# A hybrid two-layer trunk: x scaled token by token before its transpose, and the modulation vector summed in columns

## The chip, the cores and the metric

The kernel runs on one core of one Trainium2 chip. The metric is the device time of one execution in microseconds (us); lower is better. One core has TensorE (PE; its weight loads are listed as PEld), VectorE (DVE), ScalarE (ACT), GpSimd (POOL) and SyncE (SP), and each of them runs its own instructions in order and waits on semaphores for the others. DMA transfers are issued from the queues of SP, ACT and POOL.

## What is computed

One sequence of 1024 tokens by 1024 channels goes through two layers. Only the first half of layer 0, up to its attention, is touched:

```python
def ada(c, w_ada, b_ada):                 # six vectors of 1024 each
    return (silu(c) @ w_ada + b_ada)      # w_ada: 1024 x 6144
h = rms_norm(x, norm_mix) * (1 + scale) + shift
p = h @ w_in                              # 1024 x 2048: S5 | q | k | v
u = p[..., :512]                          # diagonal state-space model (S5), then a GLU
q, k, v = ...                             # 512 each: 4 heads, differential attention,
                                          # q and k normed per 64 channels and rotated
x = x + gate * (concat(s5, attention) @ w_out)
```

The first two of the six modulation vectors (shift and scale of the mixer) are needed before h; the other four (its gate, and those of the FFN) only later. All matrix products are fp32 in effect: each operand is split in a high part that TensorE takes in one pass (fp32r, names ending in hi) and the rest (lo), and a product is hi·hi + hi·lo + lo·hi, three matmuls.

## The kernel before

Activations lie channel-major: a tile `x[b]` holds 128 channels by 8 groups and 512 tokens of block b. `start` (L1071) is the first phase. `load_x` (L347) brings x in eight tiles of 128 tokens, transposes each on TensorE in 128x128 pieces (`xps`), copies the result to x (half on VectorE, half on ScalarE) and squares the token-major tile on ScalarE for the RMS sums. `mods_row` (L265) computes the first 2048 columns of the modulation as rows: the vector silu(c) is the stationary operand, one column, and 512 columns of `w_ada` stream past it (`mpr`); the four rows are copied, transposed back (`mpc`) and added to the bias (`mod`, L291), and `gm` (L302) is the norm's gain times 1 + scale. `scaled` (L1089) multiplies x by the token's 1/rms, spread over partitions through TensorE (`bc`), and `shifted` (L1095) makes `nh` = gm·xn + mod on ScalarE, its cast m0hi and its rest m0lo on VectorE. Beside it `s5_params` (L592) works out the S5 discretisation: exponentials and sines on small tiles, then powers of the 64 states by complex products (`cmul`, L678 to L683; `s5E` on VectorE, `s5D` on GpSimd), then a table `s5W` on GpSimd (L772 to L777), stored through SP's queue to `dR`, and short products `s5gp`, `s5kp` on TensorE.

`u_proj` (L1118) multiplies the first 512 columns of w_in in four blocks of 128, each for two token blocks: 24 matmuls of 128x512 for one `pu`. Weights come as 512 KB tiles `wraw`, are cast on ScalarE (`whi`, L449) and their rest is made on VectorE (`wlo`, L450). Then `attn_proj` (L914) runs twice, for two pairs of heads: for q, k and v, eight tiles `pq` of 128 tokens by 256 columns, 24 matmuls each. A q or k tile is squared (`asq`, ScalarE), summed by head (`ass`, VectorE), raised to -1/2 (`ars`, GpSimd), multiplied out of PSUM (`aqn`, L952), rotated on GpSimd and transposed (`tq`). pu and pq share two PSUM buffers. S5 quarters (`pS`, `H`, `pY`) are woven into the first attn_proj, the first attention steps (`sps`, `mx`, `po`, `os`) into the second.

The remaining 4096 modulation columns take another road, `mods_acc` (L310): a tile `mwt` of w_ada rows is multiplied by silu(c) per partition and accumulated on VectorE (`macc`, L334 and L336) over eight tiles, and TensorE sums over the partitions with a vector of ones (`mpc`, L391). 2048 of these columns stand beside u_proj in tiles of 1024, and 2048 beside the second attn_proj in tiles of 512, with two mwt buffers each.

In this part of the kernel the order on each engine is not the program's: a scheduler places the instructions by its own estimate of times, with the program's order as its preference, and may hoist one past others when its buffers are free. `weave(a, b, r)` in the program interleaves r steps of b with each step of a, `chain` runs one after the other, `lockstep` one step of each in turn. From the FFN on the order of TensorE is fixed by hand.

## Time and profile before

| | us |
|---|---|
| median of three runs | 3184.99 (3182.13 to 3188.43) |
| the profiled execution | 3195.05 |
| its span | 3192.2 |
| TensorE busy in the span | 2998.9 (94%) |
| VectorE, ScalarE, GpSimd busy | 1940.1, 1157.8, 891.2 |
| TensorE busy, 0 to 416 us | 341.10 |

The mean granted TensorE clock of the execution is 0.971 of full speed (2.4 GHz; the lower of its two levels is 1.2 GHz, a granted clock of 0.5). The chain of work that ended last is TensorE for 40% of the span and VectorE for 4%. Over the whole span TensorE is the busy engine, so an idle stretch of it is what can be won, and the first 416 us hold 75 of the 193 us of them.

A row of a timeline reads: start, duration, engine, line, operation, tile written and tiles read, count of like instructions that follow each other, and in brackets how long the engine stood idle before and for what. A wait for several things is put down to the last. A row of a group ("lines") gives the busy time, the mean of one in ns, and the idle time ahead.

### The profile page before, as it was taken

To read this page: it belongs to the slowest core of one execution; us is meant where nothing else is said; L and a number is where in the kernel's file an instruction comes from. 1 tells how busy PE (TensorE), PEld (TensorE's weight loads), DVE (VectorE), ACT (ScalarE), POOL (GpSimd) and SP (SyncE) were. 2 spreads that over 40 slices of the span, in tenths; PEclk is the share of its full clock that TensorE was granted. 3 is DMA by queue.
4 is the path that set the end of the run, shared out by engine and by line. 5 is a ranking of instruction groups with operands and counts; after the bars stand their busy time and mean duration, and the time that the engine had idled before them with its cause. 6 is when DMAs were issued, how large, how long until landed. Compare 5 with 4: busy or idle time off the path is not lost. (4 is left out here: it accounts for less than half of the span.)

```text
span 3192.2 us, 51849 instructions
## 1 busy us (share of the span) xinstructions
PE 2998.9 (94%) x19966; PEld 2242.3 (70%) x19966; DVE 1940.1 (61%) x3918; ACT 1157.8 (36%) x2318; POOL 891.2 (28%) x1002
## 2 busy tenths in 40 slices
PE   5889999998999999999999999999999999999998
PEld 2678866776777766666666777666766667777777
DVE  6854665556674646777777456467777774434443
ACT  3212443333223644343333245433434432322222
POOL 6652411001111302443443342034444334200000
PEclk7889998999999999999999999999999999999999
DMA  7753221224574442221222254422222213523332
GB/s 248 189 151 67 80 73 53 83 71 145 176 219 134 147 150 88 71 68 57 80 79 62 81 165 133 153 68 72 76 62 79 74 54 93 168 86 94 96 103 92
DMA packets 489862, 338.44 MB, mean 106 GB/s; under 512 B 44280, under 2 KB 451088, under 8 KB 488592
## 3 DMA queue, kind: packets, MB, share of 16 engines
q1 hardware_dynamic: 474288, 304.75, 32.0%
q0 software_dynamic: 7632, 25.64, 2.6%
q10 hardware_dynamic: 7696, 4.74, 0.6%
q8 instruction: 158, 2.59, 0.3%
q14 instruction: 88, 0.72, 0.1%
HBM read 292.59 MB, written 42.47 MB: 105 GB/s over the span
## 5 line engine op out<-in xcount | busy, mean ns | idle before, releaser
L449 ACT CAST whi<-wraw 128x1024 fp32r<-128x1024 f32 (+2 forms) x472 | 401.8, 852 | 897.8 <-PE pu L466 180.8
L466 PE MATMUL pd<-dd,whi 128*128 128x512 f32 x1408 | 463.3, 410 | 12.8 <-DVE x L534 7.8
L450 POOL TENSOR_TENSOR wlo<-wraw,whi 128x1024 fp32r<-128x1024 f32 (+2 forms) x184 | 325.0, 1767 | 491.0 <-ACT whi L449 467.4
L450 DVE TENSOR_TENSOR wlo<-wraw,whi 128x1024 fp32r<-128x1024 f32 (+2 forms) x288 | 298.1, 1036 | 267.6 <-ACT whi L449 252.1
L466 PE MATMUL pg<-fhi,whi 128*128 128x512 f32 x704 | 302.2, 429 | 13.4 <-DVE sg L521 10.8
L466 PEld LDWEIGHTS pd<-dd,whi 128*128 128x128 f32 x1408 | 253.8, 189 | 79.2 <-ACT whi L449 17.2
L466 PE MATMUL pu<-fhi,whi 128*128 128x512 f32 x704 | 296.4, 421 | 1.3 <-ACT ev L1360 0.6
L466 PE MATMUL pg<-fhi,wlo 128*128 128x512 f32 x704 | 282.9, 402 | 6.9 <-DVE wlo L450 6.9
L466 PE MATMUL pu<-fhi,wlo 128*128 128x512 f32 x704 | 279.8, 397 | 4.0 <-POOL wlo L450 2.4
L466 PE MATMUL pg<-flo,whi 128*128 128x512 f32 x704 | 281.9, 400 | 0.0
L466 PE MATMUL pd<-dd,wlo 128*128 128x512 f32 x704 | 279.2, 397 | 1.9 <-DVE oss L1053 1.0
L466 PE MATMUL pu<-flo,whi 128*128 128x512 f32 x704 | 278.5, 396 | 0.0
L534 DVE SCALAR_TENSOR_TENSOR x<-pd,mod,x 128x512 f32<-128x512 f32 x192 | 143.4, 748 | 123.4 <-PE pd L466 122.3
L466 PE MATMUL pkrv<-xh,whi 128*128 128x512 f32 x384 | 164.3, 428 | 12.6 <-ACT ev L1360 6.8
L466 PEld LDWEIGHTS pg<-fhi,whi 128*128 128x128 f32 x704 | 134.9, 192 | 48.6 <-DVE sg L521 12.0
L466 PEld LDWEIGHTS pg<-fhi,wlo 128*128 128x128 f32 x704 | 135.1, 192 | 40.8 <-DVE wlo L450 9.4
L466 PEld LDWEIGHTS pd<-dd,wlo 128*128 128x128 f32 x704 | 133.1, 189 | 38.4 <-DVE wlo L450 5.5
L466 PEld LDWEIGHTS pu<-fhi,whi 128*128 128x128 f32 x704 | 133.0, 189 | 37.1 <-issue 2.4
L466 PEld LDWEIGHTS pu<-fhi,wlo 128*128 128x128 f32 x704 | 133.0, 189 | 36.1 <-POOL wlo L450 3.3
L466 PE MATMUL pkrv<-xh,wlo 128*128 128x512 f32 x384 | 153.5, 400 | 2.0 <-DVE wlo L450 2.0
L466 PEld LDWEIGHTS pg<-flo,whi 128*128 128x128 f32 x704 | 135.5, 192 | 25.2
L466 PE MATMUL pkrv<-xl,whi 128*128 128x512 f32 x384 | 153.1, 399 | 0.0
(457 smaller groups left out, 6026.0 us busy)
## 6 DMA issues: line engine op xcount, KB each, us to landing
wraw<-in_ffn_w_gate SPq DMA_DIRECT2D x88, 512.0 KB, 3.9
wraw<-in_ffn_w_up SPq DMA_DIRECT2D x88, 512.0 KB, 4.0
wraw<-in_ffn_w_down SPq DMA_DIRECT2D x128, 256.0 KB, 2.7
...
kd<-ev SPq DMA_DIRECT2D x48, 256.0 KB, 2.0
...
```

What stands on the lines that cost most here:

```text
L449: nc.scalar.copy(hi, raw)
L450: (eng or nc.vector).tensor_tensor(lo, raw, hi.bitcast(F32), op=ALU.subtract)
L466: nc.tensor.matmul(out, lhsT=w(k), rhs=x(k), start=first and i == 0, stop=last and i == n - 1)
L534: nc.vector.scalar_tensor_tensor(x[:, n, :], pd, gate[:, n : n + 1], x[:, n, :], op0=ALU.mult, op1=ALU.add)
```

## The change

- `mods_row` turns its product round: pieces of w_ada of 128 rows by 128 columns are the stationary operand and silu(c) is one moving column, 128 products (two passes each) into 16 columns of one PSUM tile. The four row copies, the four transposes and the strided sum are replaced by one sum.
- `load_x` also scales the token-major tile in place by the token's 1/rms: a small operation on VectorE (`nrs`), a pow on GpSimd (`nrp`) and a scaled copy on ScalarE for each of eight tiles. `scaled`, with its 16 multiplies and the tiles xn, is dropped.
- `shifted` transposes the scaled tiles a second time (`xnp`, 64 transposes) and makes m0hi and nh from PSUM with two activations on ScalarE, so that VectorE makes only m0lo.
- `u_proj` runs two column blocks in lockstep; shifted is woven into it, and S5's parameters at one step in two.
- The eight stores of the S5 table go to GpSimd's queue.
- All 4096 later modulation columns are now in tiles of 512 with four buffers: 22 of the 64 steps beside the first attn_proj and the rest beside the second.

```diff
-        pr = self.pa.tile([P, 512], F32, tag="d", name=self.nm("mpr"))
-        row = self.tp.tile([P, 512], F32, tag="ev", name=self.nm("mrow"))
-        nc.gpsimd.memset(row, 0.0)
+        nc = self.nc
+        w = self.A["w_ada"][l]
+        pc = self.pa.tile([P, 16], F32, tag="d", name=self.nm("mpc"))
         for k in range(KT):
             for u in range(2):
                 wt = self.wp.tile([P, 1024], F32, tag=("wraw", "whi", "wlo")[(2 * k + u) % 3], name=self.nm("mwt"))
                 nc.sync.dma_start(wt, w[k * P : (k + 1) * P, u * 1024 : (u + 1) * 1024])
-                for t in range(2):
-                    q = 2 * u + t
+                for q in range(8):
                     nc.tensor.matmul(
-                        pr[32 * q : 32 * q + 1, :],
-                        lhsT=self.cact[:, k : k + 1],
-                        rhs=wt[:, t * 512 : (t + 1) * 512],
-                        start=(k == 0),
-                        stop=(k == KT - 1),
+                        pc[:, 8 * u + q : 8 * u + q + 1], lhsT=wt[:, q * P : (q + 1) * P], rhs=self.cact[:, k : k + 1],
+                        start=(k + u + q == 0), stop=(k == KT - 1), skip_group_check=True,
                     )
             yield
-        for t in range(4):
-            nc.scalar.copy(row[32 * t : 32 * t + 1, :], pr[32 * t : 32 * t + 1, :])
-        pc = self.pa.tile([P, 512], F32, tag="d", name=self.nm("mpc"))
-        for q in range(4):
-            nc.tensor.transpose(pc[:, q * P : (q + 1) * P], row[:, q * P : (q + 1) * P], self.ident)
-        nc.vector.tensor_tensor(
-            self.mod[l][:, 0:16].rearrange("p (t q) -> p t q", q=4),
-            pc.rearrange("p (q t r) -> p t q r", q=4, r=32)[:, :, :, 0],
-            self.vc1[:, 48 * l : 48 * l + 16].rearrange("p (t q) -> p t q", q=4),
-            op=ALU.add,
-        )
+        nc.vector.tensor_tensor(self.mod[l][:, 0:16], pc, self.vc1[:, 48 * l : 48 * l + 16], op=ALU.add)
         self.mods_g(l, 1)
...
             sq = self.tp.tile([P, D], BF16, tag="ev", name=self.nm("xsq"))
             nc.scalar.activation(sq, xi, AF.Square, accum_out=ss[:, t : t + 1])
+            rs = self.cp.tile([P, 1], F32, tag="nrs", name=self.nm("nrs"), bufs=2)
+            nc.vector.tensor_scalar(rs, ss[:, t : t + 1], 1.0 / D, EPS, op0=ALU.mult, op1=ALU.add)
+            rp = self.cp.tile([P, 1], F32, tag="nrp", name=self.nm("nrp"), bufs=2)
+            nc.gpsimd.tensor_tensor(rp, rs, self.mhalf[:, 0:1], op=ALU.pow)
+            nc.scalar.activation(xi, xi, AF.Copy, scale=rp[:, 0:1])
...
             for qt in range(4):
                 for i in range(2):
-                    nc.sync.dma_start(self.dR[qt][:, i], W[i][:, 4 * qt : 4 * qt + 4, :])
+                    g_.dma_start(self.dR[qt][:, i], W[i][:, 4 * qt : 4 * qt + 4, :])
...
-        def scaled(b):
-            bc = self.rstd_rows(self.rstd_pow(self.cp, ss[:, 4 * b : 4 * b + 4], 1.0 / D, EPS))
-            for k in range(KT):
-                v.tensor_tensor(xn[b][:, k, :], x[b][:, k, :], bc, op=ALU.mult)
-                yield
-
         def shifted(b):
 
             hh.append(self.big(F32R, f"m0hi{b}"))
             hl.append(self.big(F32R, f"m0lo{b}"))
             for k in range(KT):
-                t = self.tp.tile([P, TB], F32, tag="t1", name=self.nm("nh"))
-                nc.scalar.activation(
-                    t, xn[b][:, k, :], AF.Identity, bias=self.mod[0][:, k : k + 1], scale=self.gm[0][:, k : k + 1]
-                )
-                v.tensor_copy(hh[b][:, k, :], t)
-                v.tensor_tensor(hl[b][:, k, :], t, hh[b][:, k, :].bitcast(F32), op=ALU.subtract)
+                pt = self.ps.tile([P, TB], F32, tag="mm", name=self.nm("xnp"))
+                for t in range(4):
+                    nc.tensor.transpose(
+                        pt[:, t * P : (t + 1) * P], xt[2 * b + t // 2][:, t % 2, k * P : (k + 1) * P], self.ident
+                    )
+                t1 = self.tp.tile([P, TB], F32, tag="t1", name=self.nm("nh"))
+                for o in (hh[b][:, k, :], t1):
+                    nc.scalar.activation(
+                        o, pt, AF.Identity, bias=self.mod[0][:, k : k + 1], scale=self.gm[0][:, k : k + 1]
+                    )
+                v.tensor_tensor(hl[b][:, k, :], t1, hh[b][:, k, :].bitcast(F32), op=ALU.subtract)
                 yield
 
-        drain(weave(weave(self.mods_row(0), chain(self.load_x(xt, x, ss), scaled(0)), RA), self.some(s5, RF), RB))
+        drain(weave(weave(self.mods_row(0), self.load_x(xt, x, ss), RA), self.some(s5, RF), RB))
         for b in range(NB):
             for i in range(2):
                 nc.sync.dma_start(self.xs[b][:, 4 * i : 4 * i + 4, :], x[b].t[i])
+        self.m0 = hh, hl
+        sh = chain(shifted(0), shifted(1))
         if mix:
-            drain(weave(chain(weave(shifted(0), scaled(1), RD), shifted(1)), s5, RC))
-        if mix:
+            drain(self.some(sh, 2), weave(weave(self.u_proj(self.at, hh, hl), sh, 1), s5, RD))
             self.attn_consts(Scratch(self.page([P, 4 * TB], F32, "atc")))
-        self.m0 = hh, hl
+        else:
+            drain(sh)
...
-        w = {}
-        for n, b in ((0, 0), (1, 0), (0, 1), (1, 1), (2, 0), (2, 1), (3, 0), (3, 1)):
-            if not b:
-                w[n] = self.wsplit(win[:, n * P : (n + 1) * P].rearrange("(k p) n -> p k n", p=P), [P, KT, P])
-            hi, lo = w[n]
-            pu = self.pa.tile([P, TB], F32, tag="d", name=self.nm("pu"))
-            self.mm3(pu, lambda k: hi[:, k, :], lambda k: lo[:, k, :], lambda k: hh[b][:, k, :], lambda k: hl[b][:, k, :], KT)
-            ut = at.tile([P, 8, 64], F32, tag="ut", name=self.nm("ut"), bufs=2)
-            nc.scalar.copy(ut, pu.rearrange("p (c j) -> p j c", j=8))
-            nc.sync.dma_start(self.us[n][:, :, 64 * b : 64 * b + 64], ut)
-            yield
+        for n0 in (0, 2):
+            ws = [
+                self.wsplit(win[:, n * P : (n + 1) * P].rearrange("(k p) n -> p k n", p=P), [P, KT, P]) for n in (n0, n0 + 1)
+            ]
+            for b in range(NB):
+                pus = [self.pa.tile([P, TB], F32, tag="d", name=self.nm("pu")) for _ in ws]
+                yield from lockstep(*(self.mm3w(pu, *w, hh[b], hl[b], KT) for pu, w in zip(pus, ws)))
+                for n, pu in enumerate(pus, n0):
+                    ut = at.tile([P, 8, 64], F32, tag="ut", name=self.nm("ut"), bufs=2)
+                    nc.scalar.copy(ut, pu.rearrange("p (c j) -> p j c", j=8))
+                    nc.sync.dma_start(self.us[n][:, :, 64 * b : 64 * b + 64], ut)
...
-        drain(weave(self.u_proj(at, hh, hl), self.mods_acc(0, (2 * D, 4 * D), self.pz, "z", tiles, nc.sync), MR))
         self.late_vectors()
         hs = self.open("s5h", 1, side="right")
         s5 = chain(*(self.s5_quarter(n, hs) for n in range(4)))
-        drain(weave(self.attn_proj(0, at, self.pa, hh, hl), s5, 1))
+        t0 = [self.tp.tile([P, TB], F32, tag=g, name=self.nm("mwt")) for g in ("t0", "ev") for _ in range(2)]
+        t1 = [self.tp.tile([P, TB], F32, tag="t1", name=self.nm("macc")) for _ in range(2)]
+        it = iter(range(1000))
+
+        def tiles():
+            i = next(it)
+            return t0[i % 4], t1[i // 8 % 2]
+
+        mods = self.mods_acc(0, (2 * D, 6 * D), self.pz, "z", tiles, nc.sync, TB)
+        drain(weave(self.attn_proj(0, at, self.pa, hh, hl), weave(s5, self.some(mods, 22), 1), 2))
         self.close(hs)
         self.attn_pages()
         ap = self.ap = self.open("m0a", 1, side="right")
-        t0 = [self.tp.tile([P, TB], F32, tag="t0", name=self.nm("mwt")) for _ in range(2)]
-        t1 = [self.tp.tile([P, TB], F32, tag="t1", name=self.nm("macc")) for _ in range(2)]
-        it = iter(range(1000))
-
-        def tiles():
-            i = next(it)
-            return t0[i % 2], t1[i // 8 % 2]
-
-        mods = self.mods_acc(0, (4 * D, 6 * D), self.pz, "z", tiles, nc.sync, TB)
-        drain(weave(self.attn_proj(1, at, self.pa, hh, hl), weave(self.attn_steps(0, (0, 1), ap, self.pa), mods, 1.6), 2.2))
+        drain(weave(self.attn_proj(1, at, self.pa, hh, hl), weave(self.attn_steps(0, (0, 1), ap, self.pa), mods, 2), 3))
```

`mm3w` (L457) is the generator that gives the 24 matmuls of a product in eight steps, as before.

On VectorE, before, around the modulation (`mod`, and `gm` made from it), with the S5 powers s5c and s5E:

```order
L683 TENSOR_TENSOR s5E_14_158<-s5c 128x16x16
L1092 TENSOR_TENSOR xn_9_143<-x_1_135,bc_517 128x512 x4
L1092 TENSOR_TENSOR xn_10_144<-x_2_136,bc_517 128x512 x4
L678 TENSOR_TENSOR s5c<-s5E_13_157,s5t_447 128x256
L679 TENSOR_TENSOR s5c<-s5E_14_158,s5t_449 128x256
L291 TENSOR_TENSOR mod_118<-mpc_506,vc_102 128x16
L705 COPY s5B_674<-s5E_14_158 128x512
L680 TENSOR_TENSOR s5E_13_157<-s5c 128x16x16
L302 SCALAR_TENSOR_TENSOR gm_120<-mod_118,vc_102 128x8
```


and now, at the same place:

```order
L667 TENSOR_TENSOR s5c<-s5E_9_153,s5t_577 128x256
L668 TENSOR_TENSOR s5c<-s5E_10_154,s5t_579 128x256
L439 TENSOR_TENSOR wlo_671<-wraw_668,whi_670 128x1024
L669 TENSOR_TENSOR s5E_9_153<-s5c 128x16x16
L670 TENSOR_TENSOR s5c<-s5E_10_154,s5t_577 128x256
L671 TENSOR_TENSOR s5c<-s5E_9_153,s5t_579 128x256
L280 TENSOR_TENSOR mod_118<-mpc_176,vc_102 128x16
L672 TENSOR_TENSOR s5E_10_154<-s5c 128x16x16
L286 SCALAR_TENSOR_TENSOR gm_120<-mod_118,vc_102 128x8
L343 COPY x_4_138<-xps_564 128x4x128
```


What stood behind gm, the rest of the S5 powers and the wlo of the first two u weights, now stands ahead of it.

On TensorE, before, from the last u product to the first q tile (`vp` is a transpose of small vectors):

```order
L466 MATMUL pu_1424<-m0hi_169_1016,wlo_1355 128x512
L466 MATMUL pu_1424<-m0hi_169_1016,whi_1354 128x512
L391 MATMUL mpc_1388<-ones,macc_1139 32x1 x32
L466 MATMUL pu_1424<-m0lo_171_1018,whi_1354 128x512
L466 MATMUL pu_1424<-m0hi_169_1016,wlo_1355 128x512
L466 MATMUL pu_1424<-m0hi_169_1016,whi_1354 128x512
L466 MATMUL pu_1424<-m0lo_171_1018,whi_1354 128x512
L466 MATMUL pu_1424<-m0hi_169_1016,wlo_1355 128x512
L250 MATMUL vp_1499<-ident,vr_1490 128x104
L466 MATMUL pq_1521<-whi_1511,m0hi_104_534 128x256
L466 MATMUL pq_1521<-wlo_1512,m0hi_104_534 128x256
```


and now:

```order
L455 MATMUL pu_1412<-m0hi_140_809,wlo_1204 128x512
L455 MATMUL pu_1413<-m0hi_140_809,whi_1209 128x512
L455 MATMUL pu_1413<-m0lo_142_811,whi_1209 128x512
L455 MATMUL pu_1413<-m0hi_140_809,wlo_1210 128x512
L797 MATMUL pS_1657<-UT_1636,s5E_9_153 64x128 x8
L797 MATMUL pS_1666<-UT_1636,s5E_10_154 64x128 x8
L455 MATMUL pq_1592<-whi_1582,m0hi_111_638 128x256
L455 MATMUL pq_1592<-wlo_1583,m0hi_111_638 128x256
```


The column sums mpc between the u matmuls are gone, and two products pS of the first S5 quarter stand ahead of the first q tile.

On VectorE, before, ahead of the first row sums `ass` of the q tiles:

```order
L336 SCALAR_TENSOR_TENSOR macc_2850<-mwt_2848,cact,macc_2850 128x512
L336 SCALAR_TENSOR_TENSOR macc_1139<-mwt_1138,cact,macc_1139 128x1024
L334 TENSOR_SCALAR macc_1139<-mwt_1138,cact 128x1024
L336 SCALAR_TENSOR_TENSOR macc_1139<-mwt_1138,cact,macc_1139 128x1024
L323 TENSOR_TENSOR mod_118<-mpc_1388,vc_102 128x8
L251 COPY vc_103<-vp_1499 128x104
L450 TENSOR_TENSOR wlo_1518<-wraw_1515,whi_1517 128x1024
L336 SCALAR_TENSOR_TENSOR macc_1139<-mwt_1138,cact,macc_1139 128x1024
L336 SCALAR_TENSOR_TENSOR macc_2850<-mwt_2847,cact,macc_2850 128x512
L947 TENSOR_REDUCE ass_1548<-asq_1546 128x4
```


and now:

```order
L320 SCALAR_TENSOR_TENSOR macc_1574<-mwt_1573,cact,macc_1574 128x512
L318 TENSOR_SCALAR macc_1575<-mwt_1570,cact 128x512
L320 SCALAR_TENSOR_TENSOR macc_1575<-mwt_1571,cact,macc_1575 128x512
L320 SCALAR_TENSOR_TENSOR macc_1575<-mwt_1572,cact,macc_1575 128x512
L439 TENSOR_TENSOR wlo_1583<-wraw_1580,whi_1582 128x1024
L320 SCALAR_TENSOR_TENSOR macc_1575<-mwt_1573,cact,macc_1575 128x512
L439 TENSOR_TENSOR wlo_1589<-wraw_1586,whi_1588 128x1024
L320 SCALAR_TENSOR_TENSOR macc_1575<-mwt_1570,cact,macc_1575 128x512
L320 SCALAR_TENSOR_TENSOR macc_1575<-mwt_1571,cact,macc_1575 128x512
L320 SCALAR_TENSOR_TENSOR macc_1575<-mwt_1572,cact,macc_1575 128x512
L936 TENSOR_REDUCE ass_1619<-asq_1617 128x4
```


Twelve macc of 128x512 in a row have taken the place of a mixture of 128x1024 and 128x512 ones; ass follows them in both.

On VectorE, before, in the second attn_proj, with the row maxima `mx` of the attention:

```order
L323 TENSOR_TENSOR mod_118<-mpc_3217,vc_102 128x4
L334 TENSOR_SCALAR macc_2849<-mwt_2847,cact 128x512
L947 TENSOR_REDUCE ass_3189<-asq_3187 128x4
L1065 SCALAR_TENSOR_TENSOR cata_2910<-ot_3237,sub_1136,cata_2909 128x128
L336 SCALAR_TENSOR_TENSOR macc_2849<-mwt_2848,cact,macc_2849 128x512
L948 TENSOR_SCALAR ass_3189<-ass_3189 128x4
L1010 TENSOR_REDUCE mx_3258<-sps_3255 128x1
L1010 TENSOR_REDUCE mx_3274<-sps_3271 128x1
L336 SCALAR_TENSOR_TENSOR macc_2849<-mwt_2847,cact,macc_2849 128x512
```


and now, after the corresponding column sums:

```order
L307 TENSOR_TENSOR mod_118<-mpc_3155,vc_102 128x4
L318 TENSOR_SCALAR macc_1574<-mwt_1570,cact 128x512
L999 TENSOR_REDUCE mx_3179<-sps_3176 128x1
L320 SCALAR_TENSOR_TENSOR macc_1574<-mwt_1571,cact,macc_1574 128x512
L1018 RECIPROCAL r_503_3250<-l_3151 128x1
L1001 TENSOR_SCALAR nmx_3181<-mx_3179 128x1
L320 SCALAR_TENSOR_TENSOR macc_1574<-mwt_1572,cact,macc_1574 128x512
L1019 RECIPROCAL r_504_3251<-l_3183 128x1
L1038 TENSOR_SCALAR os_3189<-po_3139,r_475_3132 128x128
L320 SCALAR_TENSOR_TENSOR macc_1574<-mwt_1573,cact,macc_1574 128x512
```


The pattern is the same; there are 48 such macc in this stretch, in six blocks of eight, where there were 16 in two.

## Rows read from the trace of the kernel before

**Rows 1.** Busy time by stage, per engine; last: granted TensorE clock, DMA share, GB/s.

```profile
0.00:57.00 57.00, 33.58 (x148) 14.69 (x148) 31.03 (x129) 17.95 (x35) 25.28 (x64) 0.83 0.95 335
57.00:111.00 54.00, 35.09 (x126) 26.69 (x126) 48.47 (x82) 19.98 (x28) 43.62 (x75) 0.70 0.30 70
200.00:310.00 110.00, 102.71 (x752) 90.53 (x752) 49.04 (x111) 24.76 (x53) 33.10 (x60) 0.93 0.42 80
310.00:416.00 106.00, 104.35 (x857) 90.02 (x856) 66.19 (x194) 47.40 (x129) 41.17 (x87) 1.00 0.28 78
```

**Rows 2.** TensorE's waits, 0 to 560 us: total, times, longest.

```profile
PE pq L466 <- DVE aqn L952: 16.0, 6, 6.9
```

**Rows 3.** TensorE's timeline: start, duration, line, tiles, count, wait in brackets.

```profile
64.69 0.79 PE L466 MATMUL pu<-m0hi,whi 128*128 128x512 f32 x1 [9.60 <-ACT whi L449]
...
116.41 0.40 PE L466 MATMUL pu<-m0hi,wlo 128*128 128x512 f32 x1
116.64 0.39 PE L466 MATMUL pu<-m0hi,whi 128*128 128x512 f32 x1
...
117.64 3.76 PE L726 MATMUL s5kp<-s5D,s5B 64*32 64x16 f32 x169
122.12 2.20 PE L726 MATMUL s5kp<-s5D,s5B 64*32 64x16 f32 x87 [0.73 <-issue]
124.25 0.50 PE L466 MATMUL pu<-m0hi,wlo 128*128 128x512 f32 x1
...
148.40 1.03 PE L391 MATMUL mpc<-ones,macc 128*32 128x1 f32 x64 [8.13 <-DVE macc L336]
149.37 0.79 PE L466 MATMUL pu<-m0lo,whi 128*128 128x512 f32 x1
...
167.82 0.58 PE L466 MATMUL pq<-whi,m0hi 128*128 128x256 f32 x1 [6.86 <-DVE aqn L952]
```

**Rows 4.** VectorE's timeline from 28 to 58 us.

```profile
28.66 0.16 DVE L562 TENSOR_SCALAR ex<-ex 128x16 f32<-128x16 f32 x1
...
37.57 0.68 DVE L359 COPY x<-xps 128x512 f32<-128x512 f32 x1
38.17 0.41 DVE L678 TENSOR_TENSOR s5c<-s5b,s5t 128x256 f32<-128x256 f32 x1
38.50 0.44 DVE L679 TENSOR_TENSOR s5c<-s5b,s5t 128x256 f32<-128x256 f32 x1
...
43.73 0.84 DVE L680 TENSOR_TENSOR s5E<-s5c 128x256 f32<-128x256 f32 x1
...
57.78 0.17 DVE L302 SCALAR_TENSOR_TENSOR gm<-mod,vc 128x8 f32<-128x8 f32 x1
```

**Rows 5.** ScalarE's timeline: its first computation, and the last square of x.

```profile
22.69 0.58 ACT L359 COPY x<-xps 128x512 f32<-128x512 f32 x1 [16.11 <-DMA mwt<-in_w_ada]
...
41.01 1.06 ACT L361 ACTIVATE xsq<-xt 128x1024 bf16<-128x1024 f32 x1
```

**Rows 6.** TensorE's weight loads (PEld), timeline from 23 us.

```profile
23.32 1.57 PEld L358 LDWEIGHTS xps<-ident,xt 128*128 128x128 f32 x8 [7.97 <-ACT x L359]
...
31.28 0.86 PEld L358 LDWEIGHTS xps<-ident,xt 128*128 128x128 f32 x8 [0.86 <-issue]
```

**Rows 7.** VectorE's timeline, a sum waiting for its weights.

```profile
153.15 1.57 DVE L336 SCALAR_TENSOR_TENSOR macc<-mwt,cact,macc 128x1024 f32<-128x1024 f32 x1 [3.14 <-DMA mwt<-in_w_ada]
```

**Rows 8.** GpSimd's timeline: the S5 sums awaited, a DMA issue, a pow.

```profile
124.51 0.54 POOL L246 DMA_DIRECT2D vr<-in_od_w  x1 [17.85 <-PE s5kp L726]
...
163.45 2.08 POOL L950 TENSOR_TENSOR ars<-ass,mhalf 128x4 f32<-128x4 f32 x1 [6.51 <-DVE ass L948]
```

**Rows 9.** Groups on VectorE, 260 to 416 us; then the page's DMA issues.

```profile
L336 DVE SCALAR_TENSOR_TENSOR macc<-mwt,cact,macc 128x512 f32<-128x512 f32 x14 | 10.7, 765 | 4.5 <-DMA mwt<-in_w_ada 4.5
L450 DVE TENSOR_TENSOR wlo<-wraw,whi 128x1024 fp32r<-128x1024 f32 x8 | 9.9, 1238 | 13.9 <-ACT whi L449 13.8
...
mwt<-in_w_ada SPq DMA_DIRECT2D x32, 256.0 KB, 3.3
```

13 lines of the change are left out of this document (4 added, 9 removed).

## The prediction

> **What bounds the kernel now.** I read the windows by stage first, then TensorE's waits, then the timelines of the engines that it waits for. The change touches only the first 416 us of the profiled span of 3192.2 us; behind that the order on every engine is the old one, so the time changes by the shift with which the output projection of layer 0 begins. The windows [rows 1] show three regimes. Up to 57 us the DMA engines are busy 95% of the time. From 57 to 111 us TensorE computes 35 of 54 us, at a granted clock of 0.70. From 200 us on it is busy 102.7 of 110 and 104.4 of 106 us: there only TensorE work counts, or a new wait. What can be won before that, the waits name: 16.0 us in all of the q/k/v tiles "pq" on "aqn", which frees their PSUM buffers [rows 2], 9.60 us of the first u matmul on a weight's cast and 8.13 us of the column sums "mpc" on VectorE's accumulation "macc" [rows 3].
>
> The profiled execution took 3195.05 us, its span 3192.2, the median of the three timed runs 3184.99. I sum on the profiled one and scale by 3184.99/3195.05.
>
> **Step 1, the modulation vector comes later.** Before, VectorE made gm at 57.8 us, with the S5 powers (L678 to L683) strewn around it [rows 4]. In the new order all 48 of those operations, two casts' remainders (wlo) and three copies stand ahead of mod, and the powers start later: one of the eight new per-tile scales "nrs" sits in the exponential's chain and waits (its two buffers) for GpSimd's pow, which waits for ScalarE to have scaled tile 2, behind all eight squares. ScalarE starts at 22.7 us [rows 5]; eight squares at 1.15 us (1.06 and the reading of the sum), three copies at 0.58 and two scales at about 1.06 (the square's own duration, the same tile) make 13.1 us, so 35.8 if no tile is late; I add 3 us for late tiles: 38.9. From that point of the chain to the first power VectorE took 9.5 us (28.66 to 38.17 [rows 4]); with small waits I put the first power at 48.8 instead of 38.2. Then 48 x 0.34 us (the distance of two alone [rows 4]) = 16.3, three copies of 0.68 = 2.0 [rows 4], two wlo of 1.24 = 2.5 [rows 9], 1.5 for powers that meet GpSimd's (0.84 for 0.41 [rows 4]), 0.4 for mod and gm: **gm at about 72 us, 14 later than before**. GpSimd's own powers mostly come behind this, since the copies that feed them stand at the end of ScalarE's row. What is removed on VectorE, 16 multiplies "xn" and 16 casts "m0hi", lay beside u's waits in the stretch where VectorE was busy 48 of 54 us; 16 more scaled copies go to ScalarE, which was busy 20 of 54 us there [rows 1]. I cost both at nothing in themselves: they decide how fast TensorE is fed in step 2.
>
> The other input of mod is now the sum of 128 products with 128x128 weights and one moving column, each in two passes: 256 weight loads in place of 64 small ones. The trace has no such product; the nearest are the fp32 transposes, whose 128-column loads follow each other at 0.107 us at full clock and 0.196 at half [rows 6]. With the 64 transposes of x that is 320 x 0.107 = 34 us or 320 x 0.196 = 63 us from 23 us on, so the last sum falls between 58 and 86 us. TensorE worked at both levels there; at the middle it ends near 71. So both inputs arrive together, and I keep 72, with 66 to 87 as bounds.
>
> The Trainium skill, "TensorE: Matmul & The Clock Gate", section "LDWEIGHTS (loading the stationary operand)", gives a weight load 1/1.2 ns per column whatever its rows: by it 128 columns cost an estimated 107 ns, which the 0.86 us for eight [rows 6] agrees with, and it speaks against this part, which makes the large matrix the stationary operand for one moving column; by it alone the sum would stay as it is.
>
> **Step 2, the first u block is dense.** Before, TensorE started pu at 64.69 us and crawled: it waited for weights, scaled input and PSUM, and its first matmul took 0.79 us where 0.39 is usual [rows 3]. It had the first two column blocks and the S5 sums behind it at an equivalent of 118.8 us (the S5 sums ended at 124.25 [rows 3], less 23 matmuls of the next blocks that were done by then, at 0.235, the distance of two). Now from 74.5 (gm, one scaled copy): 96 pu x 0.235 [rows 3] = 22.6; 56 transposes "xnp" and 30 of S5 at 0.109 (0.107 by [rows 6]) = 9.4; the S5 sums "s5kp" 6.0 (3.76 + 2.20 [rows 3]); 4 us for a stretch at half clock after the idle start (some 20 pu at twice the distance). Together 42 us: **116.5, 2.3 us earlier** although it starts ten later, because weights and S5 tables lie ready. Each us by which gm moves, moves this one for one.
>
> **Step 3, no column sums between the u blocks.** The second two blocks wait at 148.40 for 8.13 us on macc, and the matmul behind it takes 0.79 us: TensorE is at half clock after the wait, up to the first q tile [rows 3]. The new order has 96 matmuls in a row: 22.6 us. Gone are 8.1 of wait and about 2 of slow clock after it. **Now 12.5 us ahead** when the q tiles begin.
>
> **Step 4, q tiles 0 to 8.** Tile 2 waits 6.86 us for aqn [rows 3]: VectorE stood in macc and in waits for its DMA (3.14 us the longest [rows 7]) ahead of the row sums "ass", and GpSimd's "ars" waited 6.51 us for those [rows 8]. The new order still has twelve macc of 128x512 ahead of ass. At 1.1 us each (four buffers, and 3.3 us from issue to landing [rows 9]) they cover 13 us, of which some lie beside u. The GpSimd chain of S5 starts 8 us earlier (it waited 17.85 us for s5kp [rows 8]), but its eight stores of W are now issued by GpSimd: 8 x 0.54 = 4.3 us, the price of its other DMA issues [rows 8], with the ars and the rotations of the next tiles queued behind them. On SyncE these stores waited for GpSimd and kept loads behind them; that is gained back. I take a loss of 2 us by tile 8, between -2 and +7.
>
> **Step 5, denser sums in the second projection.** From 200 to 416 us VectorE had 16 macc (14 of one form in [rows 9], and two that begin a sum); now 48, in six blocks of eight. 32 more at 0.765 us [rows 9] are 24.5 us on an engine that was busy 115 of 216 us [rows 1]. A block is 6.1 us, and row maxima, wlo and aqn that TensorE needs stand behind or within it. By the old ratio (9 us in which TensorE idled to 115 us busy) they cost 1.9; a third of them uncovered costs 8. I take 4, between 0 and 10. Landing isn't the limit: four buffers instead of two.
>
> **Sum.** -12.5 + 2 + 4 = -6.5: 3188.5 on the profiled one, **3178.5 us** as a median.
>
> **Rivals.** (a) *More is kept*: macc hides (step 5 at 0) and the tiles behind 8 profit from S5's earlier start: -12.5 to -18, 3167 to 3172. For it speaks that TensorE idles only 9 us in 216 [rows 1]; against it, that nothing there gets shorter. (b) *No change*: the blocks of macc cost 9 to 16 us of waits, or the loss in step 4 is 7: -3 to +4, 3182 to 3189. (c) *Slower*: the 256 weight loads run at half clock, with TensorE idle between the tiles of w_ada; the last sum is at 86, gm at 87, step 2 ends 15 later: +8.5, about 3193. It decides from gm at 79 us on. For it: the transposes at 23.3 us ran at half clock [rows 6]; against it: PE is then busier than before. (d) *The powers meet GpSimd's*: all 48 at 0.84 instead of 0.41 [rows 4] would add 21 us before gm, +14, 3199; the feeding copies come too late for more than a few. The Trainium skill, "SBUF — State Buffer", section "Who interferes with whom", states that a VectorE instruction with two SBUF inputs and a GpSimd one that reads SBUF block each other for a whole instruction; the 0.84 beside 0.41 [rows 4] agrees.
>
> **Chances.** Forecast 0.40 (-11 to -3), more kept 0.20, no change 0.20, slower by (c) or (d) 0.20. About 0.2% (6.4 us) is what timing this kernel can tell from no change. Half of the forecast's case and all of (a) lie below 3178.6: faster 0.42; the other half with most of (b): same 0.36; (c), (d) and the tail of (b): slower 0.22. The range that leaves 2 in 10 out is 3165 to 3194: down to (a) with gm at 68, up to (c).
>
> **What would show it.** Step 1: gm near 72, the last mpc of mods_row shortly before; at 80 or later (c) or (d) is right, told apart by the PE row's clock and the length of the powers. Step 2: s5kp and the first two blocks done by 117. Step 3: no wait on macc before the first pq; that at 139 to 142. Step 4: tile 2 at about 155, tile 8 near 190. Step 5: waits of pq, mpc and sps on VectorE from 200 us on, 4 us more than before; 12 or more is (b). If the output projection starts over 12.5 us earlier than before, (a).

## The result: 32 us slower, and the profile after

| | before | after |
|---|---|---|
| median, runs side by side (us) | 3185.55 (3182.13 to 3188.43) | 3217.52 (3208.11 to 3225.32) |
| ratio | | 1.0092 (95%: 1.0069 to 1.0114) |
| the profiled execution; its span (us) | 3195.05; 3192.2 | 3208.11; 3206.3 |
| first `pu`; first `pq`; tile 8 | 64.7; 151.7; 200.6 | 81.5; 152.5; 217.1 |
| second projection (tile 24); `pout` | 302.4; 419.4 | 319.0; 437.1 |

`pu`, `pq` and tiles stand for the start of their first matmul; tile 8 is the ninth `pq` tile, as they are counted from 0. `pout` is the first matmul of the output projection. The forecast was 3178.5 us. Up to `pout` the profile shows 18 us of the loss. The profiled execution of before lies 10 us above its median and that of after is the shortest of its four, so the two profiles show less than the medians. What stands behind `pout` is taken up in the last group of experiments.

The windows of after, answering [rows 1]: length, busy time of PE, PEld, DVE, ACT, POOL, granted clock, DMA share, GB/s.

```profile
0.00:57.00 57.00, 47.91 (x226) 47.53 (x226) 18.74 (x112) 19.29 (x31) 19.33 (x66) 1.00 0.86 283
57.00:111.00 54.00, 52.43 (x283) 47.31 (x283) 32.83 (x63) 33.58 (x50) 30.48 (x40) 1.00 0.29 93
200.00:310.00 110.00, 95.44 (x747) 83.90 (x748) 64.33 (x132) 22.30 (x45) 44.30 (x70) 0.91 0.53 112
310.00:416.00 106.00, 103.79 (x938) 90.66 (x937) 68.55 (x202) 41.64 (x117) 43.59 (x88) 1.00 0.38 113
```

TensorE is far busier up to 57 us (47.91 against 33.58), yet starts u later. From 57 to 111 us it works almost without a gap, as step 2 wanted. From 200 to 310 us it now idles 14.6 us where it idled 7.3: new waits. From 310 us on nothing has changed (2.2 us idle, before 1.7).

TensorE's waits from 0 to 560 us, answering [rows 2]: total, times, longest.

```profile
PE pY L831 <- DVE H L822: 11.7, 4, 5.1
PE pq L455 <- DVE wlo L439: 11.1, 2, 10.9
PE pq L455 <- DVE aqn L941: 6.6, 9, 1.9
PE tq L954 <- POOL aqn L951: 4.1, 1, 4.1
PE s5kp L715 <- POOL s5D L669: 4.0, 1, 4.0
PE pY L829 <- DVE s5tm L805: 3.8, 1, 3.8
```

The old waits are gone or small (`aqn` 16.0 to 6.6, `macc` 8.1 to nothing), and others stand in their place: on the weight's rest `wlo` of the first q tile and on S5's states `H`, both made by VectorE.

TensorE's timeline of after, answering [rows 3] (start, duration, line, tiles, count, wait in brackets):

```profile
60.95 6.83 PE L275 MATMUL mpc<-cact,mwt 128*128 128x1 f32 x32
...
81.51 0.71 PE L455 MATMUL pu<-m0hi,whi 128*128 128x512 f32 x2
...
113.46 0.95 PE L715 MATMUL s5kp<-s5D,s5B 64*32 64x112 f32 x4 [4.03 <-POOL s5D L669]
...
126.36 1.52 PE L715 MATMUL s5kp<-s5D,s5B 64*32 64x16 f32 x54 [0.56 <-issue]
...
163.84 0.58 PE L455 MATMUL pq<-wlo,m0hi 128*128 128x256 f32 x1 [10.95 <-DVE wlo L439]
174.19 0.39 PE L455 MATMUL pq<-whi,m0hi 128*128 128x256 f32 x1 [1.85 <-DVE aqn L941]
```

Its weight loads, answering [rows 6]:

```profile
60.74 6.95 PEld L275 LDWEIGHTS mpc<-cact,mwt 128*128 128x128 f32 x32
67.42 1.76 PEld L342 LDWEIGHTS xps<-ident,xt 128*128 128x128 f32 x8
```

Eight transposes take 1.76 us, twice the 0.86 that [rows 6] show at the upper level: TensorE ran at half clock. The windows print 1.00 there only because the clock record of this execution has no entry before a rise at 81 us.

VectorE's timeline, answering [rows 4] and [rows 7] (the five sums from 151.45 us in one row, then the second and third of them by themselves):

```profile
47.28 0.41 DVE L667 TENSOR_TENSOR s5c<-s5b,s5t 128x256 f32<-128x256 f32 x1
...
52.77 0.69 DVE L343 COPY x<-xps 128x512 f32<-128x512 f32 x1 [4.72 <-PE xps L342]
...
78.13 0.17 DVE L280 TENSOR_TENSOR mod<-mpc,vc 128x16 f32<-128x16 f32 x1
...
78.58 0.16 DVE L286 SCALAR_TENSOR_TENSOR gm<-mod,vc 128x8 f32<-128x8 f32 x1
...
151.45 7.99 DVE L320 SCALAR_TENSOR_TENSOR macc<-mwt,cact,macc 128x512 f32<-128x512 f32 x5
153.29 2.27 DVE L320 SCALAR_TENSOR_TENSOR macc<-mwt,cact,macc 128x512 f32<-128x512 f32 x1
155.59 2.27 DVE L320 SCALAR_TENSOR_TENSOR macc<-mwt,cact,macc 128x512 f32<-128x512 f32 x1
...
160.66 0.75 DVE L320 SCALAR_TENSOR_TENSOR macc<-mwt,cact,macc 128x512 f32<-128x512 f32 x1 [0.82 <-DMA mwt<-in_w_ada]
...
162.56 1.22 DVE L439 TENSOR_TENSOR wlo<-wraw,whi 128x1024 fp32r<-128x1024 f32 x1
...
197.30 0.69 DVE L803 TENSOR_TENSOR s5tm<-pS,s5Wq 128x512 f32<-128x512 f32 x1 [4.72 <-DMA s5Wq<-dR]
```

GpSimd's, answering [rows 8], and the groups of [rows 9] (VectorE, 260 to 416 us):

```profile
79.60 0.62 POOL L667 TENSOR_TENSOR s5w<-s5D,s5t 128x256 f32<-128x256 f32 x1 [16.52 <-ACT s5D L681]
...
152.78 2.23 POOL L761 TENSOR_TENSOR s5w<-s5W,s5t 128x1024 f32<-128x1024 f32 x1
154.97 2.34 POOL L762 TENSOR_TENSOR s5w<-s5W,s5t 128x1024 f32<-128x1024 f32 x1
172.19 1.48 POOL L939 TENSOR_TENSOR ars<-ass,mhalf 128x4 f32<-128x4 f32 x1 [14.88 <-DVE ass L937]
...
181.37 2.27 POOL L772 DMA_DIRECT2D dR<-s5W  x4
```

```profile
L320 DVE SCALAR_TENSOR_TENSOR macc<-mwt,cact,macc 128x512 f32<-128x512 f32 x39 | 29.3, 752 | 6.7 <-DMA mwt<-in_w_ada 6.4
L439 DVE TENSOR_TENSOR wlo<-wraw,whi 128x1024 fp32r<-128x1024 f32 x8 | 10.5, 1312 | 10.3 <-ACT whi L438 10.2
```

The second and third sum take 2.27 us each where one alone takes 0.75, and they stand beside GpSimd's two products of 128x1024. None of the sums up to 420 us in this trace that stand beside no computation of GpSimd's took over 0.754 us.

### The profile page after: what moved, and what is told of

Read it like the earlier page. It is cut to its first block, busy times and chain, and to the rows that moved or that the text cites. A ratio compares the mean times of both kernels' runs of the same rounds, so it can differ in the third digit from the quotient of the medians.

```text
span 3206.3 us, 52418 instructions
## 1 busy us (share of the span) xinstructions
PE 3038.7 (95%) x20210; PEld 2304.5 (72%) x20210; DVE 1916.8 (60%) x3910; ACT 1175.0 (37%) x2338; POOL 887.0 (28%) x1015
## 5 line engine op out<-in xcount | busy, mean ns | idle before, releaser
L455 PEld LDWEIGHTS pd<-dd,whi 128*128 128x128 f32 x1408 | 253.7, 189 | 78.6 <-ACT whi L438 16.4
L455 PEld LDWEIGHTS pg<-fhi,whi 128*128 128x128 f32 x704 | 135.6, 193 | 47.8 <-DVE sg L510 12.0
```

The costliest lines, as they stand in the source:

```text
L455: nc.tensor.matmul(out, lhsT=w(k), rhs=x(k), start=first and i == 0, stop=last and i == n - 1)
```

## The experiments

The ratio is to the kernel before, timed beside it on the same chip (95% interval), `pout` is read from each kernel's one profile (before 419.4, after 437.1). Seven pairs of kernels here have the same order up to `pout`, since one of the two differs only behind it; their profiles reach it 0.9 to 4.3 us apart. A difference of that size in `pout` says nothing. In the code cuts `...` stands for lines left out.

### The column form of the first modulation product (e1, e2, e5)

**e1_rows**: the changed kernel with `mods_row` as before.

```diff
-                for q in range(8):
-                    nc.tensor.matmul(pc[:, 8*u+q : 8*u+q+1], lhsT=wt[:, q*P : (q+1)*P], rhs=self.cact[:, k : k+1], ...)
+                for t in range(2):
+                    nc.tensor.matmul(pr[32*q : 32*q+1, :], lhsT=self.cact[:, k : k+1], rhs=wt[:, t*512 : (t+1)*512], ...)
```

> The changed kernel with only mods_row as before: rows of 512 columns, silu(c) as the stationary column, four copies, four transposes. Theory A (the column form is the root: its 256 weight loads of 0.209 us run at half clock, TensorE is taken from 10 to 76 us and gm comes at 78.5 us): the last row product by 55 us, transposes of x at 0.11 us again, gm at 66 to 72 (VectorE's S5 powers are then last), first u matmul at 68 to 74 instead of 81.5; q tile 0 some 8 us earlier, the whole 8 to 12 us faster than the changed kernel, about 3206 against 3217. Theory B (the root lies behind u: VectorE stands in the sums macc waiting for their DMA, with wlo of the first q weights behind them, 10.95 us of TensorE, and the S5 table comes late): the gain of the first stage is lost in a longer wait before q tile 0, and the whole is within 4 us of the changed kernel.

1.0043 (1.0025 to 1.0061), `pout` 431.9. gm is back at 56.7, the first q tile at 143.3, 8.5 us ahead of the kernel before; the lead is gone by tile 8 (213.3). Between the ratios of after and e1 lie 0.0049, 16 us, more than theory A had; that the lead is lost again is what theory B had.

**e2_colsonly**: the kernel before with the column form alone (the diff of e1 turned round).

> The kernel before with only mods_row changed to the 128 column products. Theory A: mods_row takes 8 times 6.7 us at half clock, gm comes at 75 to 80 instead of 57.8, and 10 to 17 us of it stay: 3195 to 3203 against 3185. Theory B: u is held by powers, weights and macc anyway; at most 5 us stay, under 3190.

1.0069 (1.0041 to 1.0097), `pout` 438.2: this part alone costs 0.7%, with gm at 78.1; that is 22 us (13 to 31), above the 10 to 17 expected.

**e5_wide_beside**: the changed kernel with two unread row products beside each eight column products.

```diff
+                for t in range(2):
+                    nc.tensor.matmul(pr[0:1, :], lhsT=self.cact[:, k : k+1], rhs=wt[:, t*512 : (t+1)*512], start=True, stop=True)
```

> The changed kernel with the old row products issued beside the 128 column products, 32 of 512 columns into a PSUM tile that nobody reads: more TensorE work, 14 us at full clock and 27 at half. Theory A1 (TensorE stays at half clock until 81 us because products with one moving column hardly use it): with 512 columns between them the clock rises in mods_row, a pass of a column product falls from 0.209 to about 0.107 us, x's transposes to 0.11, and eight rounds of 16 passes twice take 6 us instead of 8.4: last column product at 55 to 62, gm at 66 to 72, whole about 3205. Theory A2 (a weight load of 128 fp32 columns that isn't a transpose takes 0.209 us at either clock, or the clock stays down for another reason): rounds get 1.7 to 3.4 us longer, gm at 90 to 105, whole 3230 to 3240.

1.0119 (1.0091 to 1.0147), `pout` 443.6. Its TensorE timeline:

```profile
28.32 1.84 PE L276 MATMUL mpc<-cact,mwt 128*128 128x1 f32 x16
30.09 1.88 PE L281 MATMUL mpr<-mwt,cact 128*1 128x512 f32 x4
...
35.58 1.09 PE L347 MATMUL xps<-ident,xt 128*128 128x128 f32 x8
```

A pass now takes 1.84/16 = 0.115 us instead of 6.83/32 = 0.213, and eight transposes 1.09: beside 512-column products the same loads run at the upper level. So it is the one-column products that hold TensorE at half clock although it is busy 47.91 of 57 us. The wide products fill what that frees (gm 78.8), and the whole takes 3229 us where theory A1 had about 3205: this run shows the cause but not its price; e1 and e2 do.

### The stores on GpSimd's queue (e3, e6)

**e3_dr_sp**: the changed kernel with the eight stores on SyncE; **e6_rows_sp**: the same and `mods_row` as in e1.

```diff
-                    g_.dma_start(self.dR[qt][:, i], W[i][:, 4 * qt : 4 * qt + 4, :])
+                    nc.sync.dma_start(self.dR[qt][:, i], W[i][:, 4 * qt : 4 * qt + 4, :])
```

> The changed kernel with the eight stores of the S5 table back on SyncE's queue. Theory A: no difference beyond 4 us, the stores cost GpSimd 4.5 us beside other work. Theory B: the stores on GpSimd hold ars and the rotations of q tiles 2 to 6 (tq waited 4.06 us for GpSimd), tile 8 comes 4 to 8 us earlier: about 3211 against 3217.

1.0092 (1.0067 to 1.0118), `pout` 433.6: tile 8 starts 13.6 us earlier (203.5), and only 3.5 us of it are left at `pout`, no more than profiles of one order differ by. The median is that of the changed kernel, as theory A had it.

> The changed kernel with mods_row as before and the S5 table's stores on SyncE. Theory A+B: with mods_row as before (3200.7) q tile 0 came 8.4 us early, and by q tile 8 it stood 12.7 us late, since the second half of the table was stored only at 163.9 us, behind rotations on GpSimd. With the stores on SyncE tile 8 comes at 198 to 206, but the blocks of macc behind it take most of it back: 3193 to 3199. If the stores don't matter: 3200 to 3203.

1.0029 (1.0008 to 1.0049), `pout` 425.4. Both parts undone, and still slower than before: what is left lies in the later sums or in the rest of the change, which e8 and e12 take up.

### The later sums (e4, e7, e8, e11, e12)

**e4_sums_old**: the changed kernel with 2048 of the later columns beside u in tiles of 1024, as before, and the rest beside the second projection.

```diff
-            drain(self.some(sh, 2), weave(weave(self.u_proj(self.at, hh, hl), sh, 1), s5, RD))
+            up = weave(weave(self.u_proj(self.at, hh, hl), sh, 1), s5, RD)
+            drain(self.some(sh, 2), weave(up, self.mods_acc(0, (2 * D, 4 * D), self.pz, "z", tiles, nc.sync), 0.5))
...
```

> The changed kernel with the later modulation columns spread as before: 2048 in tiles of 1024 beside u_proj (one step per two steps of it), 2048 in tiles of 512 with two buffers beside the second attn_proj. Theory A: the wait for wlo before q tile 0 (10.95 us) shrinks, but sums between the u blocks wait again as before (8 us), and the late gm stays: 3208 to 3215 against 3217. Theory B: macc no longer stands ahead of wlo: 12 to 18 us faster, 3199 to 3205.

1.0077 (1.0049 to 1.0106), but `pout` 448.7: u, now dense, has no room for them (it ends at 190.4, with waits of 8.0 us for a weight's rest, 8.0 for `ut` and 11.0 for `m0lo` and `m0hi`). The old place does not fit the new u. The median, 3213 us, is as theory A had it.

**e7_eighth**: the changed kernel with one of eight tiles of each later sum (it leaves out the other seven, so the later modulation vectors are incomplete); **e11_before_eighth** and **e12_rows_sp_eighth** are the same edit in the kernel before and in e6.

```diff
-            for k in range(KT):
+            for k in range(KT if l else 1):
```

> The changed kernel with one of eight tiles of w_ada in each later modulation sum (the other 56 of 64 loads and multiply-adds are left out): the price of these sums where they now stand. Theory B: without them no wlo waits behind macc before q tile 0 (10.95 us) and the second projection has VectorE at its old load: 12 to 20 us faster than the changed kernel, 3197 to 3205. Theory A: TensorE's work sets the stage from 80 us on and the sums are mostly beside it: at most 6 us, 3211 to 3217.

1.0008 (0.9988 to 1.0028), `pout` 413.6, 23.5 us earlier than after. Between the ratios lie 0.0084, 27 us, more than theory B had.

> The kernel before with the first of the eight tiles of each later modulation sum alone: seven of eight loads and multiply-adds of the later 4096 columns are left out, so the later modulation vectors are not the reference's. The same removal in the changed kernel took 28 us. Theory B (the sums cost more in their new places than in the old): here it takes 8 to 16 us (the 8.1 us wait for macc between the u products, and parts of the waits for aqn), 3169 to 3177. Rival (the sums cost the same wherever they stand, some 25 us, and the change only moved the price): 3157 to 3163.

0.9989 (0.9974 to 1.0004), `pout` 402.1, 17.3 us earlier than before; the median shows 4 of them, fewer than either theory had.

> The kernel of e6_rows_sp (the change with the row form of the modulation product and the table's stores on SyncE) with the same seven eighths of the later sums left out. Theory: without both costly parts what is left (token-major scaling, blocks in step) is worth the 8 to 9 us by which the first q tile begins earlier, and no sum stands in front of a q tile: pout some 30 us earlier than before, at 385 to 395, unless a new wait (for S5's H) takes the place; against the same removal from before (e11) 6 to 12 us less. Rival (the gain up to q is lost to S5's chain, which starts no earlier): the same as e11 within 4 us.

0.9984 (0.9965 to 1.0004), `pout` 411.4: by the median the rival. It starts the q tiles at 142.3, 6 us ahead of e11 (148.3), and reaches `pout` 9 us later. TensorE's busy time up to `pout` is 16.7 us longer, its idle time 7.4 shorter. The second transposes `xnp`, busy 11.6 us, stand ahead of the q tiles, within the lead. Of the 15.3 us lost behind the first q tile 10.5 lie before tile 8 (200.3 against 195.7), and there the granted clock differs. The windows 140 to 200 us of e12 and then of e11:

```profile
140.00:200.00 60.00, 52.08 (x490) 45.66 (x489) 26.23 (x57) 11.86 (x22) 20.83 (x40) 0.77 0.53 125
140.00:200.00 60.00, 51.00 (x358) 44.87 (x359) 24.36 (x54) 11.83 (x22) 35.18 (x47) 0.91 0.48 118
```

Why the clock is lower there isn't shown; in the medians what is left of the change is worth nothing.

**e8_rows_sp_late**: e6 with the later sums multiplied by a copy of silu(c) made after the first q tile's row sums, so that no sum can stand ahead of them.

```diff
-                c = self.cact[:, k : k + 1]
+                c = (self.cact if l else self.cactl)[:, k : k + 1]
...
```

> As e6_rows_sp, and the sums macc use a copy of silu(c) that is made only after the first q tile's row sums, so that the scheduler can't put them ahead of the q weights. Theory B: the wait for wlo before q tile 0 (7.76 us with mods_row as before) goes, q tile 2 starts at 150 to 156, tile 8 at 185 to 195; the denser sums later take 5 to 8 us back: 3181 to 3190, level with the kernel before or below it. If S5 or the sums' density sets the end instead: no more than 3 us under e6_rows_sp.

1.0024 (1.0005 to 1.0042), `pout` 413.5, 5.9 us ahead of before. The first rows of a wait in the q tiles, in e6 and then in e8:

```profile
149.05 0.58 PE L471 MATMUL pq<-wlo,m0hi 128*128 128x256 f32 x1 [6.10 <-DVE wlo L455]
```

```profile
142.97 0.39 PE L471 MATMUL pq<-wlo,m0hi 128*128 128x256 f32 x1 [0.39 <-DVE wlo L455]
```

The wait for the weight's rest was the sums queued ahead of it, and without it tile 2 starts at 153.3 instead of 161.1. But a kernel that is 5.9 us ahead at `pout` ended 0.24% behind.

### What happens behind `pout` (e9, e10, e13 to e17)

At the start of the output projection TensorE waits twice some 2.2 us for `os`, and its clock falls. In the kernel before:

```profile
434.40 0.45 PE L1062 MATMUL ot<-ident,os 128*128 128x128 f32 x1 [2.17 <-DVE os L1056]
...
443.66 0.45 PE L1062 MATMUL ot<-ident,os 128*128 128x128 f32 x1 [2.25 <-DVE os L1056]
```

The windows 430 to 450 and 450 to 480 us of e8:

```profile
430.00:450.00 20.00, 16.83 (x43) 8.72 (x42) 7.66 (x26) 6.28 (x22) 1.08 (x2) 0.50 0.01 2
450.00:480.00 30.00, 28.65 (x73) 16.28 (x73) 14.31 (x38) 9.52 (x25) 3.15 (x3) 0.51 0.00 0
```

and of the kernel before:

```profile
430.00:450.00 20.00, 15.11 (x46) 8.37 (x46) 8.40 (x29) 4.74 (x18) 1.65 (x3) 0.66 0.00 0
450.00:480.00 30.00, 27.82 (x122) 17.63 (x122) 21.56 (x53) 16.23 (x39) 7.69 (x6) 1.00 0.13 36
```

In the profiles of e3, e5, e7, e8 and e12 the stretch at half clock lasts 47.8 to 51.2 us, in before, after, e1, e2, e4, e6 and e11 10.2 to 13.7.

**e9_late_fill** and **e10_before_fill**: e8, and the kernel before, with ten unread products in each of the two waits; the order of the rest stays.

```diff
+        if not b and hd == 2 and i > 1:
+            for _ in range(10):
+                nc.tensor.matmul(tp[:, 1:3, :], lhsT=self.ident, rhs=self.vt[0][:, 0, :], start=True, stop=True)
...
         nc.tensor.transpose(tp[:, 0, :], st["os"], self.ident)
```

> The kernel of e8_rows_sp_late with ten unread 128x256 products on TensorE in each of the two places at the start of the output projection where it waits some 2.2 us for os (ot, heads 2 of block 0); the order is otherwise that of e8. In e8 the output projection began 5.9 us earlier than before, but TensorE then stood at half clock for 51.2 us instead of 13.7 and the gain was lost. Theory C (the two idle stretches let the clock fall, and how long it stays down then decides the time): with them filled the granted clock stays at its upper level past pout, pg follows pout by 95 to 105 us instead of 121 to 123, and the median is 3172 to 3182, faster than before and with a spread under 10 us. Rival (the clock falls there for what the attention steps are, not for the waits): a stretch of 13.7 or some 48 us at half clock stays, the median is 3190 to 3197, the spread as in e8.

> The kernel before with the same ten unread products in each of the two waits for os, nothing else. Theory C: its stretch of 13.7 us at half clock from 434.1 us, and the one of 13.7 us at 516, go or shorten; 13.7 us at half clock cost about 6.8 us of work, of which the 4.3 us of added products lie in the two waits: 3176 to 3183, 2 to 9 us less than before. Rival: the stretch stays, 3183 to 3188.

e9 0.9998 (0.9985 to 1.0010), e10 0.9979 (0.9967 to 0.9992). e9's same windows, and the filled wait:

```profile
430.00:450.00 20.00, 19.17 (x90) 13.30 (x88) 8.58 (x33) 5.09 (x21) 1.63 (x3) 1.00 0.01 2
450.00:480.00 30.00, 27.94 (x121) 17.95 (x122) 21.12 (x52) 15.93 (x39) 7.67 (x6) 1.00 0.16 43
```

```profile
431.82 4.48 PE L1073 MATMUL ot<-vt,ident 128*128 128x256 f32 x20
```

The clock stays up, so the two waits, filled together here, are what let it fall. The median of e9 (3185.82) and its spread (18.6 us) were not as expected: the ten products take 4.48 us in a wait of 2.2, and e9's profile reaches `pout` 4.2 us later than e8's in the same order; why the executions still spread isn't shown.

**e17_before_fill5**: five products instead of ten.

> The kernel before with five unread products in each of the two waits for os in place of ten. In e9 the ten took 4.48 us in each place, twice the wait of 2.2 us that they stood in; five take some 2.24. Theory: five are enough to keep the upper clock and the surplus work goes: 3 to 5 us below e10, 0.9960 to 0.9970 of the kernel before. Rival (with five the clock falls as in the kernel before): 0.998 to 1.001.

0.9974 (0.9961 to 0.9987), 3175.47 against 3184.15 us, the fastest here that computes everything; the clock stays at 1.00 from 400 to 480 us. The first wait, filled:

```profile
427.78 2.32 PE L1064 MATMUL ot<-vt,ident 128*128 128x256 f32 x10
```

e10's interval overlaps, so that five are better than ten isn't shown.

**e13_after_fill**, **e14_before_eighth_fill**, **e15_eighth_fill**, **e16_rows_fill**: the changed kernel, e11, e7 and e1 with the waits filled as in e9, so that each part's price is read without that stretch.

> The changed kernel with the ten unread 128x256 products in each of the two waits for os at the start of the output projection (as in e9 and e10). With them the time behind pout was about 2767 us in e9 (3185.8 less 417.7) and e10 (3181.5 less 415.7). Theory C: of the 32 us by which the changed kernel is slower, 18 to 23 lie ahead of the output projection and the rest is the long stretch at half clock, which falls in part of its executions; with the waits filled the median is 437 + 2767 = 3204 (3200 to 3208), the spread under 15 us. Rival (all 32 us are in the change itself): 3213 to 3218.

> The kernel before with seven eighths of the later modulation sums left out (the later modulation vectors are not the reference's) and the two waits filled. By pout (402.1 in e11) 3169 (3165 to 3173); against e10 (3181.5) the price of the sums in their old places, 10 to 17 us. Rival (the sums' price was hidden behind the clock only by chance, and is small): 3176 to 3181.

> The changed kernel with the same seven eighths left out and the two waits filled. By pout (413.6 in e7) 3181 (3176 to 3186); against e13 the price of the sums in their new places. Theory B (the new places cost more): over 20 us, so 6 or more above the price in the old places (e10 less e14). Rival (the same price in both): within 3 us of it.

> The changed kernel with the row form of the first modulation product (as in e1) and the two waits filled. Theory A (the column form is about half of the loss): against e13 5 to 8 us less by pout (431.9 in e1, 437.1 after), so 3196 to 3200. Rival (the 17 us between the medians of the changed kernel and e1 are all due to the column form): 3185 to 3190.

The granted clock is 1.00 from 400 to 480 us in the profiles of e10 and e13 to e16. The prices of the sums are differences of the ratios, and of `pout`.

| waits filled | all later sums | one eighth of them | price of the sums |
|---|---|---|---|
| the kernel before | e10: 0.9979, `pout` 415.7 | e14: 0.9947 (0.9932 to 0.9962), 401.2 | 0.0032: 10 us; 14.5 at `pout` |
| the changed kernel | e13: 1.0074 (1.0062 to 1.0086), 440.5 | e15: 0.9965 (0.9953 to 0.9977), 409.3 | 0.0109: 35 us; 31.2 at `pout` |
| the same, row form | e16: 1.0031 (1.0018 to 1.0043), 428.4 | | |

With the clock kept up the changed kernel still loses 1.0074 less 0.9979, 0.0095 or 30 us: the rival in e13, the stretch is not what the change cost. By the intervals of the two ratios this is good to some 6 us, and so are the differences that follow. The sums in their new places cost 25 us more than in the old ones (17 at `pout`); without them the change costs 0.0018, 6 us, which the overlapping intervals of e14 and e15 don't tell from nothing. Undoing the column form takes 0.0043, 14 us (8 to 19), off e13: more than the 5 to 8 that theory A read from `pout`, and its rival's 17 isn't excluded. The executions of e16 spread over 22.6 us although its profile shows no fall of the clock. The two parts overlap: with one eighth of the sums, the row form (e12, `pout` 411.4, its stores on SyncE) is hardly ahead of the column form (e7, 413.6).

TensorE's waits from 140 to 420 us, of e13 and then of e15:

```profile
PE pY L831 <- DVE H L822: 11.7, 4, 5.1
PE pq L455 <- DVE wlo L439: 10.5, 2, 10.4
```

```profile
PE pq L455 <- DVE wlo L439: 1.1, 2, 0.7
PE pY L831 <- DVE H L822: 0.4, 1, 0.4
```

Both new waits go with the sums.

## Why the prediction was wrong, step by step

**Step 1**, the structure right, the price too low. gm came at 78.6 us (72, bounds 66 to 87). I had bounded a pass by 0.107 and 0.196 us and taken the middle, because TensorE had worked at both levels before; it ran at the lower level throughout, 6.83/32 = 0.213 us a pass, above my upper bound. That the last product came only 5 us late (76.2, not 71) was luck: I let the products begin at 23 us and they began at 10.04; 320 passes of 0.213 us from 23 us on would have ended at 91. Half clock is rival (c)'s mechanism, with gm 0.4 us short of the 79 from which I let it decide; but its idle time between the tiles of w_ada isn't there, TensorE worked without a gap from 10.04 us on. Rival (d) fell at this place: the powers took 0.42 us each (47.28), and GpSimd's began only behind them. By the Trainium skill, "TensorE: Matmul & The Clock Gate", section "LDWEIGHTS (loading the stationary operand)", a load of 128 columns takes an estimated 107 ns. The trace of e5 is near it (0.115 us a pass), that of the changed kernel pays twice as much. VectorE came to `mod` 2 us after the last product: the powers began 0.42 us apart on average where I took 0.34, and among them it had waited 4.72 us for x's transposes on the same slow TensorE and 2.5 for two casts.

**Step 2** ended at an equivalent of 127.8 instead of 116.5 us: 7 from gm, and 4.0 of a wait that I had excluded. I let GpSimd's powers follow VectorE's and did not ask who waits for them: `s5kp` did, at 113.46, as they began only at 79.60.

**Step 3** right: 96 matmuls in 22.5 us (22.6) and no wait. But 32 matmuls `pS` of S5 (150.61, 2.0 us), which I had read in the new order and not priced, stood behind them, and the first q tile began at 152.5 against 151.7 before: none of the 12.5 us of lead was left.

**Step 4** is the step that failed most. From the first q tile to tile 8 I had forecast 2 us more than before; it was 64.6 us against 48.9, 15.7 more (tile 2 at 174.2, not 155, tile 8 at 217.1, not 190; 13.3 us of both lie ahead of the first q tile). With one eighth of the sums the two stretches are 51.5 (e7) and 47.4 us (e11), so that the sums cost 13.1 us here in the new places and 1.5 in the old; in the filled kernels it is 18.2 and 0.0. I had priced the twelve sums by what stands behind the whole block, `ass`, and taken them as 13 us partly beside u. The order that I had read shows `wlo` of the first q weights between them: eight sums ran from 151.45 us on, `wlo` came behind them at 162.56, and TensorE stood 10.95 us for it.

A sum was dearer than the 1.1 us that I took (eight in 11.1 us), and not for late tiles, the reason that I gave: these made 1.3 of the 11.1 us (0.82 and 0.49 of idle time). The first three sums took 1.80, 2.27 and 2.27 us, 4.1 more than at 0.75, with 0.04 us idle between them, while GpSimd computed on the S5 table (152.78, 154.97); from 157.90 on, with GpSimd done, they took 0.75. That is the mechanism of rival (d), which I had priced for the powers alone.

The wait went further by GpSimd's order: it stood 14.88 us for the first `ass` (172.19) with the rest of the S5 table behind it, and its stores were issued at 181.37 and 189.97 (165.09 and 173.81 in e15), so that VectorE waited 4.72 us for `s5Wq` (197.30). The 11.7 us on `H`, for which I had no term, go with the sums (0.4 in e15), but how isn't shown: a sum stands close ahead of `H` on VectorE at one of the four waits (2.46 us, at 255.61), and two `wlo` at the longest (5.12, at 284.31).

At the start of the second projection (tile 24) the sums had cost 27.0 us in the changed kernel (321.8 in e13, 294.8 in e15) against 13.0 in the kernel before (298.8 in e10, 285.8 in e14). The unfilled kernels, in the same order, give 19.9 (319.0 and 299.1) and 15.7 (302.4 and 286.8): the direction is shown, the size to some 10 us.

**Step 5** within its bounds: from tile 8 to `pout` the changed kernel took 1.2 us more than before (220.0 and 218.8), and 5.2 more in e13 against e10; 4 was forecast. From 260 to 416 us VectorE had 39 sums of 0.752 us, and from 310 on TensorE still worked 103.79 of 106 us.

So the sum -6.5 became +17.7 at `pout` in the profile. Of these 24.2 us 11.3 came by steps 1 and 2, 2.0 by `pS`, 13.7 by step 4, and step 5 took 2.8 less than forecast. What was forecast as kept is there in part when gm is on time: in e1, e6 and e8 the first q tile starts 8.5 to 9.5 us earlier than before.

Not settled: why undoing the column form gives 6 us at the first q tile (144.2 in e16, 150.2 in e13) and 15.6 by tile 24, but 9.3 and 10.4 between after and e1; why the stretch at half clock behind `pout` is short in one execution and long in another; and whether the sums would be free elsewhere, since a place beside neither projection wasn't tried, nor the sums in their new place with GpSimd's table out of the way.
